# Sums of weight quarters for the second feed-forward made in other stages, and a drain of GpSimd moved

## The chip, the cores and the metric

The kernel runs on one core of a Trainium2 chip. A core has five engines with a queue each: TensorE (PE, with its weight loads as PEld), VectorE (DVE), ScalarE (ACT), GpSimd (POOL) and SyncE (SP), and DMA engines that they share. Instructions of one queue run in order; between queues there are semaphores. The metric is the device time of one execution in microseconds (us); lower is better.

## The reference, cut to what matters

One layer on 512 tokens of width 1024, all in float32: a first feed-forward, two token mixers side by side, a second feed-forward, each with a norm before and after and a residual.

```python
x = x + 0.5 * rms_norm(swiglu_ffn(rms_norm(x, norm_pre[l, 0]), ffn1_w_in[l], ffn1_w_out[l]), norm_post[l, 0])
mixed = token_mixer(rms_norm(x, norm_pre[l, 1]), w_mix_in[l], ...)
x = x + rms_norm(mixed, norm_post[l, 1])
x = x + 0.5 * rms_norm(swiglu_ffn(rms_norm(x, norm_pre[l, 2]), ffn2_w_in[l], ffn2_w_out[l]), norm_post[l, 2])
```

`swiglu_ffn` is `(silu(gate) * up) @ w_out` with `gate, up = split(x @ w_in)`; the inner width is 2816. The change touches the preparation of the second feed-forward's `w_out`.

## The kernel before, in words

**Products.** Every float32 operand is split into a high and a low part, and a product is three matmuls (high by high, high by low, low by high). ScalarE makes the high part of a weight (L279), VectorE the low part (L281). The large products use Strassen's scheme with seven products in place of eight, so they need sums of quarters of the weight matrix as well as the quarters themselves.

**Stages.** In order: the first feed-forward's first products (`ffn_in`), its last product with `w_out` (`ffn_out`), the mixers (`mixer`), the mixers' output product, the second feed-forward's `ffn_in` and `ffn_out`. `ffn_out` goes over two halves of the output columns, and in each over 11 pieces of 256 rows of `w_out` (`k2`). Eight pieces in the first half (2 to 9) and five in the second (2, 4, 3, 6, 8) are "quartered": they use sums of weight quarters. Between the halves the first half's output is scaled and its squares are summed (`post0`: squares on ScalarE L436, small column arithmetic on GpSimd L437, a multiply on VectorE L474), and the second half's banks of PSUM wait for that.

**Sums of quarters.** For `w_out` the sums are made in DRAM ahead of their use, by DMA alone (`sums_ahead`, L863 to L875): three plain copies on SyncE's queue (L869 to L871, 512 KB in all) bring three quarters of the piece into a scratch tile, then three accumulating DMAs on GpSimd's queue (L874) add to it: one of 256 KB, then two of 128 KB. Each of the three waits for the landing of the one before. There are 13 such tiles for each feed-forward. `f1sums` and `f2sums` are the names of the scratch tiles.

**When they are made.** `sums_due` (L877) sets the list of tiles that are due; every call of `make_sums` (L880) starts one tile more and takes each tile under way one step further, so that a tile needs four calls: the copies, and one call for each accumulate. The calls stand in the program's order between products. For the first feed-forward they stand in its own `ffn_in` and in the first half of its `ffn_out`. For the second, the constant `AHEAD` = 10 says that ten tiles are made in the mixers, in 13 calls (four in `job_f`, one in `job_rows`, eight in `job_t`); the last three are made in the first half of the second `ffn_out` (L998).

**GpSimd's other work.** It adds quarters of the first weights (L295), does the small arithmetic of the norms (L437, L441), masks in the mixers (`affine_select`, L1522, with the fill of `C`, L1559, ahead of it in the queue), and a `drain` between the halves of the second `ffn_out` (L1007), put behind the last of the accumulates.

**The first feed-forward's tail.** In `last`, each of four tiles of 128 tokens gets its last matmuls, the norm after the feed-forward (`post1`: L436 on ScalarE, L437 and L441 on GpSimd, L492 on VectorE), the norm before the mixers (`root`: L436, L437, L441 again, then L464 on VectorE), and a transpose on TensorE (L347) ahead of the mixers' first products (L542).

**Order.** The instructions of each engine are put in order when the program is built; weights are loaded on SyncE's queue (L242) a fixed number of pieces ahead.

Of the kernel before, what the change touches and what calls it, by code (L numbers as in the profile page):

```python
# [11 lines left out]
ALU = mybir.AluOpType  # L12
# [72 lines left out]
PLACES, LATER = {2: 1, 4: 2, 6: 0, 8: 3}, {7: (2, 3)}  # L85

AGAIN, ROWS = (10,), (18, 19, 20, 21)
EVERY, AHEAD = 5, 10

# [25 lines left out]
class Layer:  # L117
# [138 lines left out]
    def split(self):  # L256

        nc = self.nc
        it = self.items.popleft()
        raw = self.raw[it.key]  # L260
        _, a, b = raw.shape
        if it.dst:
            w = it.dst()
        else:
            if self.wt is None:
                self.wt = self.wp.tile([P, 2 * D * WBUF + FRONT + PAD], F32R, name="w")
            if not self.slot and it.key[0] != "mix":
                self.free = deque(FREE2 if it.key[0] == "f2" else FREE)
            n, o = self.lie("out" if it.key[1] == "out" else "mix" if it.key[0] == "mix" and b == 512 else "any")
            self.free.remove(n)  # L270
            w = self.wt[:, o : o + 2 * D].rearrange("p (b k t) -> p b k t", b=2, k=a)
            self.slot[id(w)] = n, o, w
        hi, lo = self.both(w)
        if it.sums:
            raw, hi, lo = (self.flat(v)[:, QUARTER:] for v in (raw, hi, lo))
        self.ready.append((w, it.dst is not None))
        rows = it.rows
        if rows is None:
            nc.scalar.copy(hi, raw)  # L279
            yield  # L280
            self.low = nc.vector.tensor_tensor(lo, raw, hi.bitcast(F32), op=ALU.subtract)  # L281
        else:
            for j in range(a):
                nc.scalar.activation(hi[:, j], raw[:, j], AF.Copy, scale=rows[:, j : j + 1])
            yield
            for j in range(a):
                nc.vector.scalar_tensor_tensor(
                    lo[:, j], raw[:, j], rows[:, j : j + 1], hi[:, j].bitcast(F32), op0=ALU.mult, op1=ALU.subtract
                )
        with self.behind(*self.hold):  # L290
            for out, other in it.adds:
                o, c = self.raw[out], self.raw[other]

                late = out[1] >= (HEAD if out[0] == "f1" else 1)
                (nc.vector if late else nc.gpsimd).tensor_tensor(o, o, c, op=ALU.add)  # L295
        self.load_due(self.done)
        self.done += 1
        yield
# [410 lines left out]
    def start(self, norm, xn):  # L709
# [8 lines left out]
        split = self.split()  # L718
        step(q[1][0], q[1][1])
        next(split)  # L720
        step(q[1][0])
        next(split)
        step(q[0][0], q[1][0])
        head = deque(HEADS)
# [56 lines left out]

    def ffn_in(self):

        if not self.second:
            self.sums_due("f1")
        for n, (p, t) in enumerate(ORDER2[len(HEADS2) :] if self.second else ORDER[len(HEADS) :]):
            if n > 14 and n % EVERY == 0 and not self.second:
                self.make_sums()
            with self.behind(*(self.c22 if p == "p3" and self.second else ())):
                self.feed()  # L790
            self.c22 = []
            self.lag()
            self.prod(p, t)
            self.after(p, t)
            if t == PAIRS - 1 and p in ("p3", "p7"):
                self.hs.append(self.h_tile(len(self.hs)))
        self.feed()
        self.lag()
# [78 lines left out]
    def sums_due(self, f, n=None, done=0):  # L877
        self.ahead, self.making = deque([k for k in self.sums_of if k[0] == f][done:n]), []

    def make_sums(self):  # L880

        if self.ahead:
            self.making.append(self.sums_ahead(*self.ahead.popleft()))
        self.making = [g for g in self.making if next(g, self) is not self]

    def ffn_out(self, gpost_row, scale, after, trans, head):
# [3 lines left out]
        nc, mm = self.nc, self.nc.tensor.matmul  # L890
# [6 lines left out]
        def more(n):  # L897
            while count[0] < min(n, len(seq)):
                half, k2 = seq[count[0]]
                count[0] += 1  # L900
                if k2 in QUARTERED[half]:
                    if k2 not in kept:
                        stay = k2 in QUARTERED[1]
                        kept[k2] = self.h_quarters(k2, PLACES.get(k2)), self.h_sums(k2, stay)
                    a, f = kept[k2]
                    made.append((a, self.s_tile(f)))
                elif half and k2 in AGAIN:
                    made.append(again.popleft())
                else:
                    made.append((self.h_tile(k2, self.x_place(*LATER[k2]) if half and k2 in LATER else None), None))  # L910
                    if not half and k2 in AGAIN:
                        again.append(made[-1])
# [21 lines left out]
        def quartered(C, M, a, s, begin):  # L934

            quarter = lambda t, j: [self.quarters(t[:, b])[j] for b in range(2)]
            A, S = (lambda j: [a[0][j], a[1][j]]), (lambda j: [s[0][j], s[1][j]])
            w = self.pull()
            product(M["p1"], A(1), quarter(w, 1), begin)
            product(C[1][1], A(3), quarter(w, 3), False)  # L940
            product(C[1][0], S(3), quarter(w, 2), False)
            self.drop(w)
            v, at = self.pull(), (1, 0, 2, 3)
            product(M["p7"], S(0), quarter(v, at[0]), begin)
            product(M["p5"], S(1), quarter(v, at[1]), begin)
            product(M["p6"], S(2), quarter(v, at[2]), begin)
            product(C[0][1], A(2), quarter(v, at[3]), False)
            self.drop(v)

        def common(M, t):  # L950

            p1, q, x, y = t
            nc.scalar.copy(p1, M["p1"])
            tt(q, M["p5"], p1, ALU.subtract)
            tt(q, M["p6"], q, ALU.add)
            tt(x, q, M["p7"], ALU.subtract)
            tt(y, M["p5"], x, ALU.subtract)
            return {(1, 1): p1, (1, 0): q, (0, 0): x, (0, 1): y}

        def add(C, T, u):  # L960
            for v in range(2):
                tt(C[u][v], C[u][v], T[u, v], ALU.add)

        def pieces(C, i):
            c = slice(QUARTER * (i // 2), QUARTER * (i // 2 + 1))
            return [(C[i % 2][v][:, c], slice(QUARTER * v, QUARTER * (v + 1))) for v in range(2)]
# [6 lines left out]
        n = 0  # L973
        for half in range(2):
            C = [[self.ps() for _ in range(2)] for _ in range(2)]
            M, T, left = None, None, len(QUARTERED[half])
            for m, k2 in enumerate(OUT[half][: PAIRS - LAST * half]):
                more(n + 2)
                h, sums = made.popleft()
                if sums:  # L980
                    begin = M is None
                    if begin:
                        M = {p: self.ps() for p in ("p1", "p5", "p7", "p6")}
                    quartered(C, M, h, sums, begin)
                    left -= 1
                    if left == 0:
                        T = common(M, [self.hf[:, j, :] for j in ROWS] if half else [self.st("c") for _ in range(4)])
                else:
                    w = self.pull()
                    more(len(seq) if half and m == PAIRS - LAST - 1 else n + 3)  # L990
                    for i in (0, 2, 1, 3):
                        for v in range(2):
                            plain(C, w, h, i, v, m == 0)
                        if i > 1 and T and m == PAIRS - 1:
                            add(C, T, i % 2)
                    self.drop(w)
                n += 1
                if half == 0 and n % 2:  # L998
                    self.make_sums()
                if n == 1:  # L1000
                    self.prod("p4", PAIRS - 1)
                    self.after("p4", PAIRS - 1)
                self.lag()
            if half == 0:
                if self.second:
                    with self.behind(self.summed):
                        nc.gpsimd.drain()  # L1007
                ys = [self.post0(pieces(C, i), g, scale) for i in range(NT)]
                self.holes()
        ws = []  # L1010
# [671 lines left out]
    def mixer(self):  # L1682
        nc, tc = self.nc, self.tc
        self.got, self.jobs = set(), deque()
        self.sums_due("f2", AHEAD)
        with tc.tile_pool(name="ma", bufs=1) as ma:
            self.vh = ma.tile([P, NT, NH, P], F32, name="vh")
            self.vm = ma.tile([P, NT, NH, 129], F32, name="vm")
# [187 lines left out]
```

## Time and profile before

| | |
|---|---|
| time, median of 3 runs | 940.39 us (939.51 to 941.82) |
| profiled execution | 939.65 us |
| its span | 937.9 us |
| TensorE busy | 923.5 us |
| VectorE busy | 758.2 us |
| ScalarE busy | 521.2 us |
| GpSimd busy | 180.9 us |

The span is the time from the first to the last instruction that the profiler recorded; the profiled execution's time holds some more around it. A time line's row is: start, duration, engine, line, operation, output<-inputs, count, and in brackets the idle time of the engine before it with the one that ended it. A `q` after an engine's name is its sequencer, which waits and issues and is not counted as busy. A view of windows gives for each stretch the busy time of the engines, the clock that TensorE was granted (1.00 is full), the mean busy share of the 16 DMA engines and what they moved in GB/s. L437 is line 437 of the kernel before.

### The profile page before, as it was taken

Reading aid. Unit: us, or ns where it says so; the run is one execution under the profiler, and the core shown is the slowest. Engines: PE = TensorE matmul, PEld = TensorE weight load, DVE = VectorE, ACT = ScalarE, POOL = GpSimd, SP = SyncE. Lnnn points to the kernel's source line nnn. Section 1 sums busy time; section 2 is a strip of 40 time slices with the busy share of each in tenths; the row PEclk is TensorE's granted clock in tenths of the full one; section 3 lists DMA queues with packets and bytes.
Section 4 is the critical chain, followed back from the end, with each engine's and each line's share of the span. In section 5 each row is a group of like instructions: output and inputs, shape, how many; then the busy total and the mean of one; then the engine's idle time right before and its main releaser. Section 6 shows DMA issues by size and latency. Waiting matters only on the chain. (4 is left out here: it accounts for less than half of the span.)

```text
span 937.9 us, 18290 instructions
## 1 busy us (share of the span) xinstructions
PE 923.5 (98%) x7435; PEld 888.1 (95%) x7435; DVE 758.2 (81%) x980; ACT 521.2 (56%) x751; POOL 180.9 (19%) x250
## 2 busy tenths in 40 slices
PE   9999999999999999999998999999999999999997
PEld 7999999999999999998886888899999999999997
DVE  6899988889887786698755564799898989988784
ACT  7645454557566467956522445495454545756551
POOL 3531112211110145223222310314000000011101
PEclk9999999999999999999998999999999999999999
DMA  9255778766996234489862124352354434379532
GB/s 320 64 156 137 193 201 192 193 147 168 246 272 202 80 110 118 116 184 205 170 115 66 46 83 136 118 180 64 118 158 135 136 113 158 105 229 279 149 117 91
DMA packets 116494, 142.28 MB, mean 152 GB/s; under 512 B 7189, under 2 KB 89657, under 8 KB 116410
## 3 DMA queue, kind: packets, MB, share of 16 engines
q1 hardware_dynamic: 101562, 126.95, 42.9%
q0 software_dynamic: 14560, 13.64, 11.4%
q8 instruction: 58, 0.95, 0.4%
q10 hardware_dynamic: 288, 0.52, 0.2%
q14 instruction: 26, 0.21, 0.1%
HBM read 138.99 MB, written 29.36 MB: 179 GB/s over the span
## 5 line engine op out<-in xcount | busy, mean ns | idle before, releaser
L279 ACT CAST w<-raw 128x1024 fp32r<-128x1024 f32 x244 | 249.4, 1029 | 195.7 <-PE ps L602 90.9
L281 DVE TENSOR_TENSOR w<-raw,w 128x1024 fp32r<-128x1024 f32 x244 | 297.3, 1222 | 30.9 <-ACT w L279 27.2
L602 PE MATMUL ps<-xq,w 128*128 128x256 f32 x2016 | 237.1, 277 | 0.0
L602 PEld LDWEIGHTS ps<-xq,w 128*128 128x128 f32 x2016 | 232.9, 188 | 0.0
L602 PE MATMUL ps<-sq,w 128*128 128x256 f32 x1512 | 178.0, 276 | 0.7 <-DVE ps L621 0.4
L602 PEld LDWEIGHTS ps<-sq,w 128*128 128x128 f32 x1512 | 174.2, 188 | 1.4 <-ACT ps L653 0.9
L295 DVE TENSOR_TENSOR raw<-raw,raw 128x1024 f32<-128x1024 f32 x72 | 89.8, 1251 | 7.4 <-DMA raw<-in_ffn_w_in_dram 5.9
L921 PE MATMUL ps<-w,hs 128*128 128x256 f32 x768 | 91.2, 276 | 0.0
L921 PEld LDWEIGHTS ps<-w,hs 128*128 128x128 f32 x768 | 88.9, 188 | 0.0
L185 PE MATMUL ps<-w,xq 128*128 128x512 f32 x192 | 78.7, 411 | 0.1
L929 PE MATMUL ps<-w,hs 128*128 128x256 f32 x624 | 75.2, 276 | 1.4 <-DVE y L474 1.4
L186 PE MATMUL ps<-w,xq 128*128 128x512 f32 x192 | 75.5, 394 | 0.0
L187 PE MATMUL ps<-w,xq 128*128 128x512 f32 x192 | 75.2, 394 | 0.0
L929 PEld LDWEIGHTS ps<-w,hs 128*128 128x128 f32 x624 | 72.7, 188 | 1.6 <-DVE y L474 1.6
L532 PE MATMUL ps<-xq,w 128*128 128x256 f32 x480 | 55.8, 277 | 0.0
L532 PEld LDWEIGHTS ps<-xq,w 128*128 128x128 f32 x480 | 54.9, 188 | 0.5 <-issue 0.5
L874 POOL DMA_DIRECT2D f2sums<-in_ffn_w_out_dram x13 | 18.2, 1460 | 191.2 <-DMA f2sums<-in_ffn_w_out_dram 190.9
L815 ACT CAST hs<-hf 128x1024 fp32r<-128x1024 f32 x34 | 35.8, 1053 | 32.9 <-PE ps L929 21.1
L816 DVE TENSOR_TENSOR hs<-hf,hs 128x1024 fp32r<-128x1024 f32 x34 | 41.5, 1222 | 9.7 <-ACT hs L815 9.3
L185 PEld LDWEIGHTS ps<-w,xq 128*128 128x128 f32 x192 | 36.5, 190 | 8.6 <-issue 1.0
L874 POOL DMA_DIRECT2D f1sums<-f1sums x26 | 22.4, 860 | 113.8 <-DMA f1sums<-in_ffn_w_out_dram 57.7
L187 PEld LDWEIGHTS ps<-w,xq 128*128 128x128 f32 x192 | 36.5, 190 | 8.3 <-DVE xq L354 0.3
(262 smaller groups left out, 1200.1 us busy)
## 6 DMA issues: line engine op xcount, KB each, us to landing
raw<-in_ffn_w_in_dram SPq DMA_DIRECT2D x98, 512.0 KB, 5.1
raw<-in_ffn_w_out_dram SPq DMA_DIRECT2D x44, 512.0 KB, 5.2
raw<-in_w_mix_in_dram SPq DMA_DIRECT2D x28, 512.0 KB, 4.0
raw<-f1sums SPq DMA_DIRECT2D x13, 512.0 KB, 7.4
raw<-f2sums SPq DMA_DIRECT2D x13, 512.0 KB, 5.6
raw<-in_w_mix_out_dram SPq DMA_DIRECT2D x8, 512.0 KB, 3.6
f1sums<-in_ffn_w_out_dram SPq DMA_DIRECT2D x26, 128.0 KB, 3.9
f1sums<-in_ffn_w_out_dram SPq DMA_DIRECT2D x13, 256.0 KB, 4.8
```

The costliest lines, as they stand in the source:

```text
L185: mm(ps, sh, mh, start=start, stop=False, **kw)
L186: mm(ps, sh, ml, start=False, stop=False, **kw)
L187: mm(ps, sl, mh, start=False, stop=stop, **kw)
L279: nc.scalar.copy(hi, raw)
L281: self.low = nc.vector.tensor_tensor(lo, raw, hi.bitcast(F32), op=ALU.subtract)
L295: (nc.vector if late else nc.gpsimd).tensor_tensor(o, o, c, op=ALU.add)
L532: mm(ps[:, u0:u1], w[:, a, k, :], self.xop(k, b, u0, u1), start=k + n + m == 0, stop=k == ND - 1 and n == 2, skip_group_check=True,)
L602: self.nc.tensor.matmul(ps[:, c], wb[b][:, k, v], left[d][:, k, :], start=first and a + n + k == 0, stop=n == 2 and k == KH - 1, skip_grou ...
L816: self.nc.vector.tensor_tensor(lo, src, hi.bitcast(F32), op=ALU.subtract)
L874: self.summed = nc.gpsimd.dma_start(to[:, a:b], v, accum_op=ALU.add)
L921: mm(out, a[kk][:, i * P : (i + 1) * P], w[:, b, kk, QUARTER * v : QUARTER * (v + 1)], start=begin and c == kk == n == 0, stop=kk == 1 and ...
L929: mm(ps[:, QUARTER * c : QUARTER * (c + 1)], A[a][:, c], B[b], start=begin and c == n == 0, stop=n == 2, skip_group_check=True,)
```

## The change

Of the 13 tiles of `f2sums`, five are made in the second half of the first feed-forward's `ffn_out`, in six calls that start up to two tiles each; seven in the mixers; one in the first half of the second `ffn_out`. The drain goes to the second feed-forward's first products, behind GpSimd's last addition of weight quarters there. In the built program the instructions of TensorE, VectorE and ScalarE stand in the same order as before; on SyncE's queue 15 copies of `f2sums` move in among the last loads of the first `w_out`, and on GpSimd's queue 15 accumulates move in between the last L437 of `post0` and the first L437 of `post1` of the first feed-forward.

```diff
-EVERY, AHEAD = 5, 10
+EVERY, EARLY, AHEAD = 5, 5, 12
...
-                (nc.vector if late else nc.gpsimd).tensor_tensor(o, o, c, op=ALU.add)
+                added = (nc.vector if late else nc.gpsimd).tensor_tensor(o, o, c, op=ALU.add)
+                if not late:
+                    self.added = added
...
     def ffn_in(self):
...
+            if n == 14 and self.second:
+
+                with self.behind(self.added):
+                    nc.gpsimd.drain()
...
-    def make_sums(self):
-
-        if self.ahead:
+    def make_sums(self, n=1):
+
+        for _ in range(min(n, len(self.ahead))):
             self.making.append(self.sums_ahead(*self.ahead.popleft()))
         self.making = [g for g in self.making if next(g, self) is not self]
...
-                if half == 0 and n % 2:
-                    self.make_sums()
+                if half == 0 and n % 2 or half and m and not self.second:
+                    self.make_sums(1 + half)
...
             if half == 0:
-                if self.second:
-                    with self.behind(self.summed):
-                        nc.gpsimd.drain()
+                if not self.second:
+                    self.sums_due("f2", EARLY)
...
-        self.sums_due("f2", AHEAD)
+        self.sums_due("f2", AHEAD, EARLY)
```

`make_sums(n)` starts up to `n` tiles and steps all that are under way; `behind` puts an instruction behind another in the order.

More of the change, by code (lines that the diff above doesn't have):

```diff
@@ L782, in ffn_in @@
     def ffn_in(self):
+        nc = self.nc
         if not self.second:
```

## Prediction

> **What bounds the kernel now.** I read the page's busy times first, then the waits of TensorE, then the time lines and windows around each wait. The page's first part gives engine, busy time, share of the span and instructions:
>
> ```profile
> span 937.9 us, 18290 instructions
> PE 923.5 (98%) x7435; PEld 888.1 (95%) x7435; DVE 758.2 (81%) x980; ACT 521.2 (56%) x751; POOL 180.9 (19%) x250
> ```
>
> TensorE is busy 98% of the span, and the change leaves the order on TensorE, VectorE and ScalarE as it was: only GpSimd's and SyncE's queues differ. So the time can move only where TensorE stands still. Two of its waits, from the view of waits (total us, times, longest us):
>
> ```profile
> PE ps L1496 <- DVE pT L1532: 4.3, 1, 4.3
> PE ps L929 <- DVE y L474: 1.4, 1, 1.4
> ```
>
> The first is in the mixers. The time line shows what stands behind it (start, duration, engine, line; in brackets the idle time before and its releaser):
>
> ```profile
> 496.97 0.81 POOL L874 DMA_DIRECT2D f2sums<-f2sums  x1 [2.53 <-DMA f2sums<-f2sums]
> 497.82 1.39 POOL L1559 MEMSET C<- 128x1548 f32 x1
> 499.17 2.42 POOL L1522 TENSOR_SCALAR_AFFINE_SELECT e<-e 128x512 f32<-128x512 f32 x4
> 499.86 1.29 DVE L1532 SCALAR_TENSOR_TENSOR pT<-ps,e 128x512 f32<-128x512 f32 x2 [9.86 <-POOL e L1522]
> ...
> 500.61 0.79 PE L1496 MATMUL ps<-nm,selr 36*128 36x512 f32 x1 [4.34 <-DVE pT L1532]
> ```
>
> Read it upwards: TensorE waits for pT on VectorE, pT for the masks of L1522 on GpSimd, and these stand in GpSimd's queue behind the last accumulate of the tenth tile, which waited for the landing of the one before it. The windows of two microseconds show a second price (stretch, length, busy time of five engines, then granted clock, DMA share, GB/s):
>
> ```profile
> 498.00:500.00 2.00, 0.00 (x0) 0.00 (x0) 0.14 (x1) 0.00 (x0) 2.00 (x3) 0.64 0.47 66
> 500.00:502.00 2.00, 1.39 (x5) 0.96 (x5) 2.00 (x5) 0.56 (x1) 1.59 (x3) 0.50 0.00 0
> 502.00:504.00 2.00, 2.00 (x7) 1.61 (x6) 2.00 (x4) 0.02 (x1) 0.00 (x0) 0.50 0.12 17
> 504.00:506.00 2.00, 2.00 (x6) 1.24 (x5) 1.43 (x4) 0.62 (x2) 0.00 (x0) 0.66 0.71 245
> ```
>
> The idle time begins at 500.61 - 4.34 = 496.27. A mean of 0.64 over 498 to 500 is a half from 498.56 on, 2.3 us later; 0.66 over 504 to 506 is a half until 505.36. From 500.61 that is 4.75 us of work at half speed, 2.4 us lost.
>
> The second wait is at the middle of the last product:
>
> ```profile
> L1007 POOLq DRAIN  x1: 8014/8014/8014, 873.9 to 873.9; - x1
> ```
>
> ```profile
> 882.02 0.19 POOL L437 TENSOR_SCALAR col<-col 128x1 f32<-128x1 f32 x1 [7.30 <-issue]
> 882.24 0.38 ACT L436 ACTIVATE junk<-ps 128x256 f32<-128x256 f32 x1 [5.59 <-POOL col L437]
> ...
> 882.75 0.98 DVE L474 TENSOR_TENSOR y<-ps,gpost 128x256 f32<-128x256 f32 x2 [5.64 <-ACT junk L436]
> ...
> 883.23 1.65 PE L929 MATMUL ps<-w,hs 128*128 128x256 f32 x12 [1.37 <-DVE y L474]
> ```
>
> The drain holds GpSimd 8.0 us, ScalarE's squares run out of small columns, and TensorE waits 1.37 us for a bank.
>
> **Part by part.** *Mixers, ten tiles to seven.* Seven tiles end in GpSimd's queue where this row stands:
>
> ```profile
> 466.68 0.81 POOL L874 DMA_DIRECT2D f2sums<-f2sums  x1 [2.94 <-DMA f2sums<-f2sums]
> 467.21 1.48 POOL L874 DMA_DIRECT2D f2sums<-in_ffn_w_out_dram  x1
> 472.51 0.85 POOL L874 DMA_DIRECT2D f2sums<-f2sums  x1 [3.82 <-DMA f2sums<-in_ffn_w_out_dram]
> 475.94 0.81 POOL L874 DMA_DIRECT2D f2sums<-f2sums  x1 [2.58 <-DMA f2sums<-f2sums]
> ```
>
> GpSimd is then free at 467.5 and the masks no longer wait for it. The idle 4.34 us goes, and with it the drop of the clock. Of its 2.4 us I take 2.0: next late is VectorE's chain through L1588, for which TensorE waits 0.4 us already. Bounds 4.3 and 6.7 us; taken: 6.3 us gained. Nine issues on SyncE go as well; loads were not what ended a wait of TensorE there, so nothing for them.
>
> Beside the first of these rows stands a rule of the Trainium skill, page "TensorE: Matmul & The Clock Gate", "Part 1: The HAM clock gate": the clock halves after an idle window of about 3.4 us and comes back after about 3.4 us of work. The trace agrees on the half, but fell after 2.3 us and took 4.75 us to come back; by the page the second price would be an estimated 1.7 us instead of 2.4.
>
> *The drain.* It goes from the middle of the last product: 1.37 us gained (below, nothing if another wait takes its place; in the first feed-forward no wait of TensorE is listed at the same middle). At its new place in the second feed-forward's first products GpSimd stands idle:
>
> ```profile
> 825.68 1.25 POOL L874 DMA_DIRECT2D f2sums<-in_ffn_w_out_dram  x1 [176.24 <-DMA f2sums<-in_ffn_w_out_dram]
> ```
>
> 8.0 us of 176 us: nothing, unless those instructions were needed, and nothing of GpSimd is queued behind it until the sums. Two tiles fewer on SyncE and GpSimd in the last product: nothing, since no other wait of TensorE is there. The program's last drain now has three accumulates behind the moved one; at most 8.0 us for all 78, so 0.3 us by share, and I take 0.
>
> *Five tiles in the first feed-forward's second half.* Added there: 15 loads on SyncE and 15 accumulating DMAs on GpSimd. All 15 stand in GpSimd's queue ahead of the first norm of the tail (L437), which before came here:
>
> ```profile
> 322.45 0.27 POOL L437 TENSOR_SCALAR col<-col,col 128x1 f32<-128x1 f32 x1 [36.34 <-ACT junk L436]
> ```
>
> So this adds a wait like the one removed. Behind it are the norms of all four token tiles, for these VectorE's L464, and for L464 TensorE's transposes:
>
> ```profile
> 327.64 1.43 DVE L464 SCALAR_TENSOR_TENSOR xn<-xs,col,gpre 128x512 f32<-128x512 f32 x2 [2.06 <-POOL col L441]
> ...
> 333.13 1.43 DVE L464 SCALAR_TENSOR_TENSOR hf<-xs,col,gpre 128x512 f32<-128x512 f32 x2 [2.06 <-POOL col L441]
> ```
>
> ```profile
> 332.45 1.03 PE L347 MATMUL ps<-ident,xn 128*128 128x128 f32 x8
> ...
> 336.15 1.04 PE L347 MATMUL ps<-ident,hf 128*128 128x128 f32 x8
> ```
>
> The first transposes have 332.45 - 329.07 = 3.4 us to spare, the second 336.15 - 334.56 = 1.6 us. If GpSimd is free at T instead of 322.45, it is late by L = T - 322.45, and from the second transposes on TensorE is late by L - 1.6.
>
> When is T? GpSimd's order pairs the tiles: first accumulates of tiles 2 and 3, then their second and third ones mixed with the first of 4 and 5, then 6. Each accumulate of a tile waits for the landing of the one before, so the shortest way through the queue is first, second, third of tile 2, then of 4, then of 6: three steps from a first to a second accumulate (a), three from a second to a third (b), two passages of 0.53 us (466.68 to 467.21) and 0.81 us for the last issue. The start: SyncE is past its last load of first-half sums at 291.8, and in the mixers the first accumulate came 5.6 us after the loads began:
>
> ```profile
> 291.42 0.34 SPq L242 DMA_DIRECT2D raw<-f1sums  x1
> ```
>
> ```profile
> 390.24 0.51 SPq L869 DMA_DIRECT2D f2sums<-in_ffn_w_out_dram  x1
> ```
>
> ```profile
> 395.87 1.24 POOL L874 DMA_DIRECT2D f2sums<-in_ffn_w_out_dram  x1 [14.64 <-DMA f2sums<-in_ffn_w_out_dram]
> ```
>
> So it starts at 297.4. Fastest: a = 5.3 and b = 3.4 (467.21, 472.51, 475.94 above). Slowest:
>
> ```profile
> 857.92 1.48 POOL L874 DMA_DIRECT2D f2sums<-in_ffn_w_out_dram  x1
> 866.99 0.85 POOL L874 DMA_DIRECT2D f2sums<-f2sums  x1 [7.58 <-DMA f2sums<-in_ffn_w_out_dram]
> 873.91 0.81 POOL L874 DMA_DIRECT2D f2sums<-f2sums  x1 [6.06 <-DMA f2sums<-f2sums]
> ```
>
> a = 9.1, b = 6.9. In the first feed-forward's own first half:
>
> ```profile
> 265.43 1.48 POOL L874 DMA_DIRECT2D f1sums<-in_ffn_w_out_dram  x1
> 273.87 0.85 POOL L874 DMA_DIRECT2D f1sums<-f1sums  x1 [6.96 <-DMA f1sums<-in_ffn_w_out_dram]
> 280.71 0.81 POOL L874 DMA_DIRECT2D f1sums<-f1sums  x1 [5.98 <-DMA f1sums<-f1sums]
> ```
>
> a = 8.4, b = 6.8. How full the DMA engines are:
>
> ```profile
> 304.00:308.00 4.00, 4.00 (x38) 4.00 (x37) 2.83 (x4) 2.93 (x4) 0.00 (x0) 1.00 1.03 302
> 308.00:312.00 4.00, 4.00 (x38) 4.00 (x37) 3.65 (x4) 2.85 (x3) 0.00 (x0) 1.00 0.66 204
> 312.00:316.00 4.00, 4.00 (x37) 4.00 (x37) 4.00 (x6) 0.20 (x1) 0.00 (x0) 1.00 0.01 2
> ```
>
> Up to 312 they are full or near it before any of the new traffic; after it they are free. So I take the first-half durations for the first tile (15.3), the middle between these and the fastest for the second (12.0), the fastest for the third (8.7): T = 297.4 + 15.3 + 12.0 + 8.7 + 1.1 + 0.8 = 335.3, and L = 12.9 us. By the fastest T = 325.5 (L = 3.1), by the slowest 297.4 + 48.0 + 1.9 = 347.3 (L = 24.9).
>
> At T = 335.3 TensorE waits at the first transposes from 332.45 to 341.9. That is long enough for the half clock: 4.75 us pass over 2.4 us of the 3.7 us of work up to the second transposes, which come at 348.0 instead of 336.15 (their data at 347.4): 11.9 us lost. Bounds: 1.5 us by the fastest, about 24 by the slowest. The late loads of the same half are behind the same DMAs; I give them no price of their own, since TensorE held up by them would wait less at the transposes.
>
> **The sum.** -6.3 - 1.4 + 11.9 = +4.2 us. The profiled execution took 939.65 us (span 937.9 and 1.75 around it), 0.74 under the median of the runs shown, 940.39; the sum made on the first gives 943.9, on the median 944.6. I forecast the median: 944.6 us. It breaks even where the tail loses 7.7 us, at a T of about 331.
>
> **Rivals.**
> 1. *The chain of accumulates is short enough* (not slower). It decides at T = 331, a little over half way from the fastest to my T. For it: before 304 the engines had gaps, and two tiles on the way at once hide part of each other's latency. Against it: the order on GpSimd has six landings in a row, and even the fastest rows overrun 322.45. At the fastest, 1.5 us are lost: 940.39 - 7.7 + 1.5 = 934.2. Chance 0.27 for T from 325 to 331 (934 to 940).
> 2. *The chain ends ahead of the tail*: all is gained, 940.39 - 7.7 = 932.7. It needs T under 324, faster than any row of the chain. Chance 0.05. The Trainium skill, page "DMA: Bandwidth & Descriptors", section "Anatomy of one DMA — SWDGE (gpsimd) path", speaks for it: 2.0 us plus bytes over 436 GB/s, an estimated 2.3 us for 128 KB, would end the chain near 314. The trace disagrees: its shortest step is 3.4 us.
> 3. *The slow rows hold to the end* (T over 343): 952 to 957. For it: 15 loads of DRAM to DRAM come on top. Against it: the engines are empty after 312. Chance 0.10.
> 4. *Another wait takes the place of GpSimd's masks in the mixers*: only 1.4 us gained, 940.39 - 1.4 + 11.9 = 950.9. Against it: VectorE idles 9.86 us there for GpSimd alone. Chance 0.05.
>
> **How the numbers follow.** My case (T from 331 to 343, 940 to 952): 0.53, likeliest 944.6. The range leaves out rival 2, rival 3 and a little at the fast end of rival 1, about 0.18: 934.5 to 951.5. A measurement of this kernel tells 0.3%, 2.8 us, from no change: faster is under 937.6 (T under 328: 0.18 of rival 1, all of rival 2), 0.23; within is T from 328 to 334 (0.09 of rival 1, 0.18 of mine), 0.27; slower, 0.50.
>
> **What would show it.** In the profile after: no wait of TensorE on pT and no half clock near 500; none at the last product's middle; L1007's drain gone and one of about 8 us early in the second feed-forward, with nobody behind it. In the first feed-forward's tail: the third accumulate of tile 6 issued near 334.5, L437 right behind it, TensorE's wait at L347 some 9 us long with a half clock behind. I am wrong if that last accumulate is issued before 327, or if TensorE waits at L347 for something else.

## The result and the profile after

The changed kernel takes 950.7 us (median of 9 runs, 948.8 to 953.0). The kernel before, run beside it, takes 941.75 us (9 runs, 939.5 to 949.1). The ratio is 1.0092, with a 95% interval of 1.0067 to 1.0118. The forecast was 944.6 us, slower, in a range of 934.5 to 951.5. The profiled execution took 949.59 us, 9.94 more than that of before. Every line behind L295 has moved by a few: the norm's L437 is now L439, L464 is L466, the transposes' L347 are L349, L542 is L544, the accumulates' L874 are L881, the products' L921 are L928, and in the mixers L1496 is L1502.

From the page of the kernel after, span and busy times (engine, busy us, share, instructions):

```profile
span 947.9 us, 18293 instructions
...
PE 926.3 (98%) x7435; PEld 891.5 (94%) x7435; DVE 760.0 (80%) x980; ACT 521.4 (55%) x751; POOL 180.2 (19%) x250
```

The instructions are three more than before; TensorE has the same 7435, and its busy time went up by 2.8 us, net of the half clock that went in one place and came in another. The waits of TensorE in the kernel after (total us, times, longest us):

```profile
PE ps L349 <- DVE xn L466: 6.4, 1, 6.4
PE ps L928 <- DVE hs L823: 4.4, 1, 4.4
...
PE ps L544 <- ACT w L279: 1.4, 1, 1.4
PE ps L604 <- DVE ps L623: 0.8, 1, 0.8
```

The two old waits, 4.3 us on pT and 1.4 us on y, are gone, as forecast. In their place stand 6.4 us at the first feed-forward's tail transposes, where some 9 were forecast, and two that were not forecast: 4.4 us earlier in the same product, for h on VectorE (`hs`, the two parts of the product's other operand), and 1.4 us behind the tail, for weights. The time line of GpSimd in the kernel after:

```profile
297.48 1.19 POOL L881 DMA_DIRECT2D f2sums<-in_ffn_w_out_dram  x1 [11.61 <-DMA f2sums<-in_ffn_w_out_dram]
...
307.24 0.84 POOL L881 DMA_DIRECT2D f2sums<-f2sums  x1 [7.04 <-DMA f2sums<-in_ffn_w_out_dram]
...
316.81 0.81 POOL L881 DMA_DIRECT2D f2sums<-f2sums  x1 [6.29 <-DMA f2sums<-f2sums]
317.34 1.48 POOL L881 DMA_DIRECT2D f2sums<-in_ffn_w_out_dram  x1
...
327.65 1.65 POOL L881 DMA_DIRECT2D f2sums<-f2sums  x2 [2.04 <-DMA f2sums<-in_ffn_w_out_dram]
328.92 1.58 POOL L881 DMA_DIRECT2D f2sums<-in_ffn_w_out_dram  x1
...
339.49 0.81 POOL L881 DMA_DIRECT2D f2sums<-f2sums  x1 [2.81 <-DMA f2sums<-f2sums]
340.06 0.91 POOL L439 TENSOR_SCALAR col<-col,col 128x1 f32<-128x1 f32 x2
```

This is the chain of the prediction, tile by tile: 297.48 to 316.81, 317.34 to the second tile's last issue (the second of the two from 327.65, at 328.4), 328.92 to 339.49. GpSimd comes to the tail's first norm at 340.06, which was 322.45 before and 335.3 in the forecast. All the waits in brackets are for landings. What follows on TensorE, in its own time line:

```profile
322.06 2.50 PE L928 MATMUL ps<-w,hs 128*128 128x256 f32 x10 [4.43 <-DVE hs L823]
...
346.03 1.94 PE L349 MATMUL ps<-ident,xn 128*128 128x128 f32 x8 [6.41 <-DVE xn L466]
...
352.24 1.04 PE L349 MATMUL ps<-ident,hf 128*128 128x128 f32 x8
...
357.49 6.11 PE L544 MATMUL ps<-xq,w 128*128 128x256 f32 x48 [1.38 <-ACT w L279]
```

The same matmuls began at 317.71, 332.45, 336.15 and 340.03 before, so TensorE is late by 4.4, 13.6, 16.1 and 17.5 us. The 16.1 at the second transposes is L - 1.6 with the measured L of 340.06 - 322.45 = 17.6 us: the prediction's formula holds. Behind the first of these waits the half clock brings the 4.4 to 7.0, and the wait at the transposes is 6.4 us because TensorE comes to it 7.0 us late already. The half clock is in the windows of 4 us of the kernel after (the last three columns are granted clock, DMA share and GB/s):

```profile
320.00:324.00 4.00, 1.94 (x9) 1.94 (x10) 4.00 (x7) 1.01 (x1) 0.92 (x1) 0.59 1.19 189
324.00:328.00 4.00, 4.00 (x22) 4.00 (x22) 2.07 (x2) 0.00 (x0) 1.20 (x2) 0.56 0.55 82
...
344.00:348.00 4.00, 1.97 (x10) 2.00 (x11) 2.88 (x6) 1.01 (x6) 2.50 (x5) 0.57 0.00 0
348.00:352.00 4.00, 4.00 (x22) 4.00 (x22) 1.94 (x4) 3.33 (x10) 2.26 (x6) 0.57 0.00 0
```

The clock falls twice, once behind each of the two waits. Where it was a half in the mixers, it stays up:

```profile
502.00:506.00 4.00, 4.00 (x17) 2.83 (x17) 4.00 (x8) 2.26 (x4) 1.93 (x2) 1.00 0.00 0
```

From TensorE's time line of the kernel after, the mixers and the end of the program:

```profile
513.47 0.48 PE L1502 MATMUL ps<-nm,selr 36*128 36x512 f32 x1
...
518.87 0.39 PE L186 MATMUL ps<-w,xq 128*128 128x512 f32 x1
...
940.88 0.84 PE L928 MATMUL ps<-w,hs 128*128 128x256 f32 x6
```

These began at 500.61, 508.17 and 930.96 before. So the lateness goes from 17.45 to 12.86 by the wait and to 10.70 by the clock: 6.75 us gained. At the end it is 9.92; between them 0.86 are lost at L604 (a wait that was 0.4 us before) and 1.66 gained where the drain stood.

### The profile page after: what moved, and what is told of

The parts are those of the page before. It is cut to its first block, busy times and chain, and to the rows that moved or that the text cites. A ratio compares the mean times of both kernels' runs of the same rounds, so it can differ in the third digit from the quotient of the medians.

```text
span 947.9 us, 18293 instructions
## 1 busy us (share of the span) xinstructions
PE 926.3 (98%) x7435; PEld 891.5 (94%) x7435; DVE 760.0 (80%) x980; ACT 521.4 (55%) x751; POOL 180.2 (19%) x250
## 4 chain that ended last, share of the span: by engine, by line
PE 51%; DVE 5%; issue 2%; DMA 2%; POOL 1%; ACT 1%; DVEq 0%; POOLq 0%; ACTq 0%
PE ps L604 13%; PE ps L936 7%; PE ps L534 6%; PE ps L928 5%; PE ps L185 5%; PE ps L187 5%; PE ps L186 5%; DVE w L281 2%; DMA raw<-in_ffn_w_in_dram 2%; PE ps L1354 2%; DVE raw L295 1%; PE ps L349 1%; POOL raw L295 1%; PE ps L544 1%; DVE ps L623 0%
## 5 line engine op out<-in xcount | busy, mean ns | idle before, releaser
L604 PE MATMUL ps<-xq,w 128*128 128x256 f32 x2016 | 237.1, 277 | 0.0
L604 PEld LDWEIGHTS ps<-xq,w 128*128 128x128 f32 x2016 | 232.9, 188 | 0.0
L604 PE MATMUL ps<-sq,w 128*128 128x256 f32 x1512 | 178.1, 276 | 1.2 <-DVE ps L623 0.8
L604 PEld LDWEIGHTS ps<-sq,w 128*128 128x128 f32 x1512 | 174.3, 188 | 2.1 <-ACT w L279 1.0
L928 PE MATMUL ps<-w,hs 128*128 128x256 f32 x768 | 94.2, 281 | 4.4 <-DVE hs L823 4.4
L295 DVE TENSOR_TENSOR raw<-raw,raw 128x1024 f32<-128x1024 f32 x72 | 89.9, 1252 | 8.6 <-DMA raw<-in_ffn_w_in_dram 7.0
L928 PEld LDWEIGHTS ps<-w,hs 128*128 128x128 f32 x768 | 91.7, 193 | 4.6 <-DVE hs L823 4.6
L936 PE MATMUL ps<-w,hs 128*128 128x256 f32 x624 | 75.0, 276 | 0.0
L936 PEld LDWEIGHTS ps<-w,hs 128*128 128x128 f32 x624 | 72.7, 188 | 0.0
L881 POOL DMA_DIRECT2D f2sums<-in_ffn_w_out_dram x13 | 18.6, 1493 | 203.2 <-DMA f2sums<-in_ffn_w_out_dram 202.8
L823 DVE TENSOR_TENSOR hs<-hf,hs 128x1024 fp32r<-128x1024 f32 x34 | 41.6, 1222 | 11.2 <-ACT hs L822 10.6
L881 POOL DMA_DIRECT2D f1sums<-f1sums x26 | 22.4, 860 | 113.2 <-DMA f1sums<-in_ffn_w_out_dram 59.7
```

Source lines behind the costliest of these rows:

```text
L295: added = (nc.vector if late else nc.gpsimd).tensor_tensor(o, o, c, op=ALU.add)
L604: self.nc.tensor.matmul(ps[:, c], wb[b][:, k, v], left[d][:, k, :], start=first and a + n + k == 0, stop=n == 2 and k == KH - 1, skip_grou ...
L823: self.nc.vector.tensor_tensor(lo, src, hi.bitcast(F32), op=ALU.subtract)
L881: self.summed = nc.gpsimd.dma_start(to[:, a:b], v, accum_op=ALU.add)
L928: mm(out, a[kk][:, i * P : (i + 1) * P], w[:, b, kk, QUARTER * v : QUARTER * (v + 1)], start=begin and c == kk == n == 0, stop=kk == 1 and ...
L936: mm(ps[:, QUARTER * c : QUARTER * (c + 1)], A[a][:, c], B[b], start=begin and c == n == 0, stop=n == 2, skip_group_check=True,)
```

## Two theories and the experiments

*Theory.* The tail's loss is GpSimd's queue: the norms stand behind fifteen accumulates, each waiting for a landing. *Rival.* It is the DMA engines: copies and accumulates hold up the weight loads of the same product, TensorE is late for that alone, and the queue only seems to be what ends last. Both waits are in the trace, so the runs take the queue away, then the accumulates, and vary the number of early tiles; none takes the late weights away and leaves the queue. The kernel before took 942.2 us beside the runs with the drain alone, two early tiles, the norms on VectorE and the other six tiles elsewhere, and 940.9 us beside the other four; each ratio is to the one beside it.

**The drain alone** (no early tiles, ten in the mixers, three in the last product):

```diff
-EVERY, EARLY, AHEAD = 5, 5, 12
+EVERY, EARLY, AHEAD = 5, 0, 10
```

> Only the drain is moved; ten tiles stay in the mixers, three in the last product, none in the first feed-forward. Theory (a moved drain frees the middle of the last product, nothing is late next): TensorE's wait of 1.4 us at L929 goes, the wait on pT in the mixers stays at about 4.3 us, no wait at the transposes of the first tail; 1.4 us under the kernel before. Rival (the last accumulates still end behind the sums of squares and take the drain's place): no change. Rival (accumulates behind the drain make the program's last drain long): the last drain, 0.66 us before, takes over 3 us and the time is up to 1 us over the kernel before.

Measured: 942.9 us, ratio 1.000 (0.998 to 1.002). On TensorE the drain's gain is there: lateness falls by 1.66 us at 883. The program's last drain takes 1.4 us, and from TensorE's last matmul to the end of the span it is 6.4 us as before. The median neither shows nor excludes a gain of that size, and this profile tells why one has to look at the step and not at the total. Its wait in the mixers, with the same ten tiles as before, is twice as long:

```profile
PE ps L1502 <- DVE pT L1538: 8.8, 1, 8.8
```

GpSimd's time line of the same kernel:

```profile
498.53 0.85 POOL L881 DMA_DIRECT2D f2sums<-f2sums  x1 [5.43 <-DMA f2sums<-in_ffn_w_out_dram]
501.90 0.81 POOL L881 DMA_DIRECT2D f2sums<-f2sums  x1 [2.52 <-DMA f2sums<-f2sums]
```

On GpSimd's time line the tenth tile's last accumulate is issued at 501.90, where it was 496.97 before, and the masks stand behind it. The landings of the same ten tiles differ by 5 us between two profiles. So the mixers' wait was 4.3 us in one execution and 8.8 in another.

**Two early tiles** (two in the first feed-forward, nine in the mixers, two in the last product):

```diff
-EVERY, EARLY, AHEAD = 5, 5, 12
+EVERY, EARLY, AHEAD = 5, 2, 11
```

> Two tiles in the first feed-forward's second half, nine in the mixers, two in the last product, drain moved. Theory (the loss is GpSimd's queue reaching the tail's norms late): the first norm of the tail is not held up (the sixth accumulate is issued near 318, the norm comes near 322), TensorE does not wait at the first transposes, the mixers' wait is gone (the ninth tile was through at 486 before, the masks are due at 486): 6 to 8 us under the kernel before. Rival (the loss is the DMA engines being full, so that weights come late): a wait of TensorE of 1 to 3 us with a late load near 317 stays, 3 to 5 us under the kernel before.

Measured: 933.25 us (931.7 to 935.3), ratio 0.9908 (0.9889 to 0.9927), faster than both kernels, and 9.0 us under the one before where the theory said 6 to 8 (in the profiled executions 7.2). On GpSimd's time line the chain ends ahead of the first norm:

```profile
317.45 0.81 POOL L881 DMA_DIRECT2D f2sums<-f2sums  x1 [2.14 <-DMA f2sums<-f2sums]
322.26 0.26 POOL L439 TENSOR_SCALAR col<-col,col 128x1 f32<-128x1 f32 x1 [4.00 <-ACT junk L438]
```

In the brackets of the norm stands ScalarE, which makes its data, and no landing. The only waits of TensorE in this profile:

```profile
PE ps L181 <- POOL ident masks.py:199: 1.6, 1, 1.6
PE ps L604 <- DVE ps L623: 1.4, 2, 0.9
```

The tail loses nothing, the mixers gain 6.75 us with nine tiles too, and the drain 1.66. So the two gains of the prediction are real, and what made the change slower is the number of early tiles.

**Three and four early tiles**, with nine and eight in the mixers and one in the last product (the edit for three; for four it is 5, 4, 12):

```diff
-EVERY, EARLY, AHEAD = 5, 5, 12
+EVERY, EARLY, AHEAD = 5, 3, 12
```

> Three tiles in the first feed-forward's second half, nine in the mixers, one in the last product. Theory (each step of the chain of accumulates in GpSimd's queue is added to the tail once the chain passes the tail's first norm): with two early tiles GpSimd's last accumulate was issued at 317.4, and a third tile adds its three steps behind the second accumulates, so T, the time at which GpSimd is free for the first L439, is about 327 and the tail loses L - 1.6 = 3 us against two tiles: 936 to 937 us. Rival (the late weight loads alone set the loss, whatever the queue): the copies of the third tile stand ahead of the weight loads as in the change itself, so the tail loses the 7 to 8 us which the kernel with the norms on VectorE lost: about 941 us.

> Four tiles early, eight in the mixers, one in the last product. Theory: the fourth tile goes side by side with the third, so T is about 331, the tail loses L - 1.6 = 7 us by the queue, and the sum is near no change: 939 to 942 us, which is the point that the prediction called its break-even. Rival (loss by the number of transfers, not by the queue's length): five tiles lost 17.5 us and two lost nothing, so four lose two thirds of it, 11.7 us: about 945 us.

Measured: 935.1 us with three, ratio 0.994 (0.991 to 0.997), and 941.8 us with four, ratio 1.0007 (0.9992 to 1.0022). The totals are the theory's to within 2 us, not the rivals', and GpSimd's queue ends within about 1 us of where it said, with three at 326.22:

```profile
326.22 0.91 POOL L439 TENSOR_SCALAR col<-col,col 128x1 f32<-128x1 f32 x2
```

and with four at 332.13:

```profile
332.13 0.91 POOL L439 TENSOR_SCALAR col<-col,col 128x1 f32<-128x1 f32 x2
```

But the totals came out right for a reason that is only half the theory's. TensorE's waits with four have none at the transposes:

```profile
PE ps L928 <- DVE hs L823: 4.8, 1, 4.8
...
PE ps L544 <- ACT w L279: 1.0, 1, 1.0
PE ps L928 <- ACT hs L822: 0.9, 1, 0.9
```

The tail of four lost 9.2 us, of which 8.4 were lost by 321, with the late weights and their half clock. The queue's L - 1.6 = 8.1 us was covered by them. With three, 2.9 us were lost to the weights and L - 1.6 = 2.2 was covered.

**The norms on VectorE.** The change, with the column arithmetic of the norms in the first feed-forward's last product on VectorE, where a reciprocal stands for the reciprocal root (so the scale of these norms is another):

```diff
-            nc.gpsimd.tensor_scalar(m, ss, s2 / D, b, op0=ALU.mult, op1=ALU.add)
+            (nc.vector if self.cols else nc.gpsimd).tensor_scalar(m, ss, s2 / D, b, op0=ALU.mult, op1=ALU.add)
...
+        if self.cols:
+            self.pow = nc.vector.reciprocal(r, b)
...
```

> The changed kernel, with the small column arithmetic of the norms in the first feed-forward's tail on VectorE instead of GpSimd (and a reciprocal in place of the reciprocal root there, so the values are others); the same 15 copies and 15 accumulates at the same places. Theory (17 us lost in the tail are GpSimd's queue): TensorE's wait of 6.4 us at the first transposes goes and the rest of the tail with it; the late weights near 317 stay (4.4 us and about 2.4 us of half clock), so the tail loses 7 us instead of 17.5 and the time is about 10 us under the changed kernel, within 2 us of the kernel before. Rival (the DMA engines are what is late, GpSimd's place in the queue tells nothing): the tail still loses over 13 us and the time is within 3 us of the changed kernel.

Measured: 939.3 us, ratio 0.9966 (0.9951 to 0.9981); 11 us less than the change took beside its own kernel before. All fifteen accumulates are still there, and the wait at the transposes is gone (L931 is the change's L928 here):

```profile
PE ps L931 <- DVE hs L826: 4.6, 1, 4.6
PE ps L181 <- POOL ident masks.py:199: 1.6, 1, 1.6
PE ps L607 <- DVE ps L626: 1.3, 1, 1.3
...
```

So the rival alone falls: with the same DMA traffic the tail loses 7.4 us instead of 17.7. The theory alone falls too: with the queue out of the way 7.4 us stay, all of them at the late weights. The total is 2.9 us under the kernel before, about 1 us beyond the theory's bound. ScalarE's time line shows the weight that came late, here:

```profile
315.30 1.05 ACT L279 CAST w<-raw 128x1024 fp32r<-128x1024 f32 x1 [7.03 <-DMA raw<-in_ffn_w_out_dram]
```

and in the change:

```profile
314.50 1.05 ACT L279 CAST w<-raw 128x1024 fp32r<-128x1024 f32 x1 [6.82 <-DMA raw<-in_ffn_w_out_dram]
```

Before, this cast began at 308.16. How a late weight makes h late is in VectorE's time line of the change: VectorE waits for the high part of this weight, and the h that TensorE waits for stands behind it in VectorE's queue.

```profile
315.58 1.22 DVE L281 TENSOR_TENSOR w<-raw,w 128x1024 fp32r<-128x1024 f32 x1 [6.93 <-ACT w L279]
...
320.79 1.22 DVE L823 TENSOR_TENSOR hs<-hf,hs 128x1024 fp32r<-128x1024 f32 x1
```

**Copies without accumulates.** The change, but the fifteen accumulates of the early tiles are left out, so that the sums of these five tiles are not made:

```diff
...
-            self.summed = nc.gpsimd.dma_start(to[:, a:b], v, accum_op=ALU.add)
+            if not self.skip:
+                self.summed = nc.gpsimd.dma_start(to[:, a:b], v, accum_op=ALU.add)
...
```

> The change with the fifteen accumulating DMAs of the five early tiles left out: their copies stay, so the sums of these tiles are not made. Theory: GpSimd's queue is empty and the DMA engines carry only the copies, so the first norm of the tail comes when its own data come, there is no wait at the transposes, and what is left of the tail's 17.5 us is what the copies alone do to the late weight loads: 0 to 4 us, in all 934 to 938 us. Rival (the copies standing ahead of the weight loads make them late by themselves): the tail loses 7 to 8 us as with the norms on VectorE, about 940 us.

Measured: 935.1 us, ratio 0.992 (0.990 to 0.995). The tail loses 2.6 us, in two waits of about 1 us on the late weights:

```profile
PE ps L929 <- DVE w L281: 1.2, 1, 1.2
...
PE ps L929 <- DVE hs L823: 0.9, 1, 0.9
```

So, against the 7.4 us with the norms on VectorE, the copies alone make about a third of the late weights' cost, and the accumulates the rest. How it comes about is seen in SyncE's time line of the change:

```profile
302.21 0.49 SPq L878 DMA_DIRECT2D f2sums<-in_ffn_w_out_dram  x1
303.80 2.15 SPq L242 DMA_DIRECT2D raw<-in_ffn_w_out_dram  x2
```

In before's time line of SyncE the group of four weight loads was one row:

```profile
294.64 6.35 SPq L242 DMA_DIRECT2D raw<-in_ffn_w_out_dram  x4
```

The last two of the four now stand behind copies, at 303.8 and later. And the engines are full from then on, in the windows of the change:

```profile
308.00:312.00 4.00, 4.00 (x37) 4.00 (x37) 0.65 (x1) 0.00 (x0) 0.89 (x2) 1.00 0.99 262
312.00:316.00 4.00, 4.00 (x38) 4.00 (x37) 0.42 (x1) 1.50 (x2) 0.00 (x0) 1.00 1.09 309
```

Before, the last of these had a DMA share of 0.01. What the accumulates add is the engines' load and not a later issue: with the copies alone these two loads are issued from 304.50 and the cast begins at 311.76; with the norms on VectorE, where the accumulates are there, they are issued from 304.17 and the cast begins at 315.30. How much of the copies' own 2.6 us is the later issue and how much the fuller engines, no run tells apart.

**The other six tiles elsewhere** (seven in the mixers, none early; the other six in the second feed-forward's first products, one step every five products):

```diff
...
-        if not self.second:
-            self.sums_due("f1")
+        self.sums_due("f2" if self.second else "f1", None, AHEAD if self.second else 0)
...
```

> No tile in the first feed-forward, seven in the mixers, the other six in the second feed-forward's first products, where GpSimd stands idle for 176 us, none in the last product; drain moved. Theory: both waits of before are gone and none comes, 8 us under the kernel before (the gains alone, 6.6 in the mixers and 1.5 in the last product). Rival (the DMA engines have no room there either): weights of the first products come late, TensorE waits there for VectorE or ScalarE, and 2 us or more of the 8 are given back.

Measured: 940.7 us, ratio 0.9988 (0.9970 to 1.0006). TensorE waits for nothing of GpSimd's there, and still 7.0 us are lost between 700 and 776, about as much as the mixers give: 4.3 us of waits, some 1.7 us by a half clock (a granted clock of 0.57 from 760 to 764), and about 1 us that is not accounted for. It is the late weights again, here on VectorE, which works on them between its evictions of TensorE's banks. Its time line:

```profile
749.73 1.23 DVE L295 TENSOR_TENSOR raw<-raw,raw 128x1024 f32<-128x1024 f32 x1 [3.53 <-DMA raw<-in_ffn_w_in_dram]
```

and TensorE's waits:

```profile
PE ps L604 <- DVE ps L623: 4.3, 3, 2.1
```

So the second cause is not one of the tail alone: beside this stream of weights, too, the DMAs make it late.

**No drain** (the change without it):

```diff
-                with self.behind(self.added):
-                    nc.gpsimd.drain()
+                pass
```

> The change without the moved drain. Theory: the drain's new place costs nothing, so nothing changes up to the last product; the program's last drain then stands behind all accumulates, at 0.08 us for each some 6 to 7 us instead of 0.9, of which about 3 are hidden by the wait for the last stores: 952 to 955 us. Rival: the loss of 0.7 us at 775, which every kernel with the moved drain shows, is that drain's: it goes here, and the end costs nothing: about 950 us.

Measured: 952.2 us (4 runs), ratio 1.0108 (1.0080 to 1.0136). The change had 1.0092 (1.0067 to 1.0118) beside its own kernel before; the intervals overlap, so the totals don't decide and the trace has to. The program's last drain, in the view of its line (count, shortest, median and longest ns, first and last start):

```profile
L1877 POOLq DRAIN  x3: 38/93/5502, 943.8 to 949.9; - x3
```

Its longest is 5.5 us, against 0.9 in the change, and the time from TensorE's last matmul group to the end of the span grew by 1.3 us: over 3 of the 4.6 us were hidden, as the theory said. The 0.7 us at L604 near 775 stay without the drain, so the rival falls. But for the kernel with the other six tiles elsewhere and the one with three early tiles, which has none, this wait is between 0.4 us (before) and 1.4 us; its variation was not tracked down. This run also lost 1.9 us between 345 and 450 at a granted clock of 1.00 and without a listed wait, which the change did not; that stays open, and the total's fit to the theory's 952 to 955 us rests on it in part.

## Why the prediction was right, and where its sizes were off

The loss of the tail, from the starts of the same matmul at 317.0, 321 and 345 in each trace against before. T is the start of the first L439; L is T - 322.45.

| early tiles | T | L - 1.6 | lost to late weights | tail in all |
|---|---|---|---|---|
| two | 322.3 | none | 0.0 | 0.0 |
| three | 326.2 | 2.2 | 2.9 | 3.0 |
| four | 332.1 | 8.1 | 8.4 | 9.2 |
| five, the change | 340.1 | 16.0 | 7.3 | 17.7 |
| five, norms on VectorE | no queue | none | 7.7 | 7.4 |
| five, copies only | no queue | none | 2.6 | 2.6 |

The last column is the larger of the two before it to within 0.3 us, and 0.8 and 1.7 us more with four and five, which waited for the weights of L544 too. So the two losses overlap and don't add. That the queue alone would have cost its L - 1.6 is the formula's; no run has the queue without the late weights.

1. *The mixers*, forecast -6.3: measured -6.75, wait and half clock both. Right.
2. *The drain*, forecast -1.4: measured -1.66. At its new place it takes 7.1 us and nobody waits. Right. At the program's end, forecast 0: the drain there went from 657 to 922 ns, and from TensorE's last row to the end of the span it is 7.0 us in both kernels. Right.
3. *The tail's mechanism*, L - 1.6 with the first transposes, half clock and second transposes: right for the change, to 0.1 us. The wait that it names came out as 6.4 us and not 9, though L was larger than forecast, since the late weights had taken 7.0 us before it.
4. *The size of T* is the step that was off: 335.3 forecast, 340.06 measured. The first tile took 19.3 us instead of 15.3, the second 11.1 instead of 12.0, the third 10.6 instead of 8.7. The prediction took the durations of the first half for the first tile, and took the engines as empty after 312, because they were before; but the change's own traffic, and the weights that it pushed back, filled that stretch (share 1.09 instead of 0.01). With two early tiles alone the first tile took 16.6 us already (297.88 to 314.50). The first tile had a = 9.8 and b = 9.6, over the prediction's slowest, a = 9.1 and b = 6.9. That pair was not the slowest at hand: the trace of before has a = 9.7 and b = 7.1 in the first feed-forward's own first half (issues at 248.15, 257.82 and 264.89), and b = 8.2 in the mixers (401.92 to 410.09). T came 4.8 us later than forecast for all this, and the loss was larger by as much.
5. *Late weights at no price*: true of the sum in the change, where the queue was the longer one, and wrong as a rule. They alone would have cost 7 us; with four early tiles they decide. And behind the tail they cost 1.4 us at L544, which the prediction did not have.
6. *The break-even* at T of about 331: the kernel with four early tiles has T = 332.1 and a ratio of 1.0007. Right, though there the weights and the queue came out alike by chance.

Together: -0.2 (ahead of 317) + 17.7 - 6.75 + 0.86 - 1.66 = 9.9 us on the profiled executions, where +4.2 was forecast; 4.8 of the 5.7 between them are T's, 1.4 L544's and 0.9 L604's; the larger gains and the 0.6 us by which the forecast went over its own L - 1.6 take some back. On the medians it is 9.0 us; one reason may be the mixers' wait that goes, which was 8.8 us in the profile with the drain alone and 4.3 in that of before, but no run shows how often it is the longer one. The forecast's sign and mechanism were right and its size was not: the 9.0 us are over twice the 4.2 forecast. The time lies 0.8 us under the upper end of the range, and T = 340.06 in the prediction's own case of 331 to 343. The total by itself would have suited rival 4 as well, at 950.9; that is chance, for the wait in the mixers, which that rival kept, is gone from the trace.

Against the fast-chain rival with the Trainium skill's formula, the runs are clear. The Trainium skill, page "DMA: Bandwidth & Descriptors", section "Anatomy of one DMA — SWDGE (gpsimd) path", gives an estimated 2.3 us for 128 KB. By the same formula 256 KB take an estimated 2.6 us. The trace disagrees: in the view of DMA issues from 296 to 312 (KB each, median us from issue to landing), the copies and accumulates of the change take

```profile
f2sums<-in_ffn_w_out_dram SPq DMA_DIRECT2D x6, 128.0 KB, 10.2
...
f2sums<-in_ffn_w_out_dram POOLq DMA_DIRECT2D x2, 256.0 KB, 9.9
...
f2sums<-f2sums POOLq DMA_DIRECT2D x2, 128.0 KB, 8.6
```

GpSimd's two rows, the ones that the formula is for, have 9.9 and 8.6 us. The Trainium skill, same page, section "Queues, rings and completion order", says that each DMA engine takes turns between the queues that have work for it. No run here shows the turns themselves. What the runs show is that SyncE's copies alone cost the tail 2.6 us, and GpSimd's accumulates beside them about 5 more.

## What to carry to other kernels

Work that is moved to an idle queue is not free for that: ask what comes next on the same queue, when, and how long each landing takes under the traffic that the move itself makes, not under that of the trace before. A chain of dependent DMAs in front of an engine's small work is to be counted in landings; here two tiles fitted and the third did not, and trying smaller numbers gave a kernel 0.9% under the one before, where five were 0.9% over. And when two waits lie in one place, take each away by itself: the larger hides the other, and a change that removes only one gains only the difference.

## What the hardware showed that was not expected

The last drain's length goes with the number of GpSimd's accumulates since the drain before it: 0.66 us with none, 0.92 with three, 1.17 with six, 1.42 with nine, 2.15 with eighteen, that is some 0.083 us for each; with all 78 it took 5.5 us, where that line gives 7.1. In the second feed-forward's first products it took 5.9 us behind 60 accumulates, in both kernels that have 60 there, and 7.1 us behind 75:

```profile
L795 POOLq DRAIN  x1: 7124/7124/7124, 657.7 to 657.7; - x1
```

The clock fell to a half behind waits of 4.4 us and of 6.4 us alike, so that in the change the same product paid for it twice. By the windows shown it stayed there about 6.8 us each time, as it had in the mixers of the kernel before; with the drain alone, behind the wait of 8.8 us, it stayed 10.2 us (granted clocks of 0.52, 0.50 and 0.70 in the three windows of 4 us from 500 to 512).
